# Moving the backward direction's 32x32 substitutions from VectorE to GpSimd, and sharing the output buffers of keys and values

## The chip, the cores and the metric

The kernel runs on one core of a Trainium2 chip. The metric is the time of one execution on the device in microseconds (us); a measurement is the median of several runs. Engines are named as in the profile: PE is TensorE (with PEld, its weight loads), DVE is VectorE, ACT is ScalarE, POOL is GpSimd, and SP is SyncE, whose queue issues nearly all the DMAs. Instructions of one engine run in the order of its program. That order is fixed when the kernel is built: a scheduler lays the instructions out by its own timeline, and in the attention phase the order on PE is the order of the code.

## The reference

One encoder block over 2048 tokens of width 1024. After a norm and one input projection (`z = h @ w_in`), two mixers work side by side, latent attention and a gated linear recurrence that runs once forward and once backward over the tokens. Then come a merge, routing, and 32 experts.

```python
def rwkv_branch(...):
    ...
    y_f = wkv7_scan(r_h, decay_h[:, :, 0], k_dir[:, :, 0], v_h, -kk, kk * a_h[:, :, 0])
    y_b = fl(wkv7_scan(fl(r_h), fl(decay_h[:, :, 1]), ..., fl(-kk), fl(kk * a_h[:, :, 1])))
    ...
def step(state, inp):
    sa = jnp.einsum('bhvk,bhk->bhv', state, a_t)
    state = state * w_t + sa[..., None] * b_t + v_t[..., None] * k_t
    return state, jnp.einsum('bhvk,bhk->bhv', state, r_t)
```

The kernel does the recurrence in chunks of 64 tokens. Each chunk needs the inverse of a unit triangular 64x64 matrix, for 8 heads, 32 chunks and 2 directions.

## The kernel before

**Phase 1** (`phase1`) computes z in column chunks. For each chunk of 128 columns `load_w` (lines 130 to 137) loads the weights, ACT rounds them to `whi`, POOL subtracts to get `wlo` (L136), and PE runs 24 matmuls per 512 tokens (`z_mm`, L143 to L145). The last eight chunks (the gates) run for one block of 512 tokens after the other, and three other pieces of work are threaded between their matmuls:

- `up_kv` and `up_q` project queries, keys and values (matmuls into `u`, copies by DVE and ACT, then a DMA to DRAM). Keys are copied by DVE into `kt` (L586, L587), values by ACT into `vm` (L597, L598), two buffers each.
- `Rwkv.inverses` inverts the triangular matrices in eight **units**, one for each pair (g, d) of a head group g = 0..3 and a direction d (0 forward, 1 backward), in the order (0,0), (0,1), (1,0), ... At most two are live.

One unit (`Rwkv.inverse`) loads the 32x32 diagonal blocks `a` by a DMA on SP's queue (L883), transposes them on DVE (L890), masks them on POOL (L891) and sets the diagonal. Then come **30 substitution steps**: step s multiplies a column by a row into `it` (L898, n*s elements with n = 31 - s) and adds that into `x` (L900), each instruction waiting for the one before. Two DVE transposes follow (L904 into `a`, L905 into `tb`). Then the **tail**: two halves of 16 blocks, each with copies by ACT (L913), 64 small matmuls (L919), a copy (L922), 64 small matmuls (L928), a copy (L931) and a DMA that stores `tt`. The tiles `a`, `of` and `x` exist once for each direction; `it`, `tb`, `tt`, `pe` and the PSUM bank `sa` exist once for both. Because `it` is one buffer, the two live units take turns in their substitutions. Because `a` is used again by the tail, the next unit of a direction loads its `a` only when the tail of the unit before has ended.

**Phase 2** starts with attention's operands for the first head (keys `kh`, `kl`, queries `qhi`, `qlo`, split by ACT and POOL), 16 matmuls for row maxima (L664), and the first scores (L684 to L686, exponentials by ACT at L689, sums on POOL and DVE at L692 and L694). Then the recurrence `rwkv` runs in between the blocks of attention. Its tiles (pool "rw") take the memory of the units' pool, which is closed when the last unit is done; so its loads (L830, L946 to L951, L854) are issued after the last store of `tt`.

```python
        live, todo = [], iter(divmod(u, 2) for u in range(8))
            if len(live) < 2 and (age >= 24 or not live):
        tmp = p.tile([128, 256], F32, name="it", bufs=1)
```

Of the kernel before, what the change touches and what calls it, by code (L numbers as in the profile page):

```python
# [9 lines left out]
F32 = mybir.dt.float32  # L10
# [4 lines left out]
OP = mybir.AluOpType  # L15
# [97 lines left out]
def phase1(k):  # L113

    nc, tc, I, S = k.nc, k.tc, k.I, k.scratch
    with ExitStack() as ctx:
# [142 lines left out]
        with k.psu as k.psu:  # L259
            for b in range(NB):  # L260
                if b == 1:
                    side, more = ExitStack(), 5
                    ups = up_kv(k, side)
                elif b == 2:
                    on(ups, 1000)
                    side.close()
                    side, more = ExitStack(), 2
                    ups = up_q(k, side)
                for j in range(LAST, len(CHUNKS)):
                    load_w(j)  # L270
                    z_out(j, b)
                    on(aside, INV)
                    if b:
                        on(ups, more)
                hx[b].close()
            on(ups, 1000)
            side.close()
            on(aside, 1000)
# [217 lines left out]
def split(k, hi, lo, src, eng=None):  # L496

    k.nc.scalar.copy(hi, src)  # L498
    (eng or k.nc.vector).tensor_tensor(lo, src, hi.bitcast(F32), op=OP.subtract)  # L499


def up_bank(k):
    return k.psu.tile([128, 512], F32, name="u", bufs=3)


def up_w(k, ctx, n, c):

    nc, tc, I = k.nc, k.tc, k.I
    wp = ctx.enter_context(tc.tile_pool(name=n + "w", bufs=1, side="right"))
    whi = wp.tile([128, c, 1024], F32R, name=n + "hi")  # L510
    wlo = wp.tile([128, c, 1024], F32R, name=n + "lo")
    for j in range(c):
        for u in range(2):
            raw = wp.tile([128, 512], F32, name="raw", bufs=RAW)
            sl = slice(u * 512, u * 512 + 512)
            nc.sync.dma_start(raw, I[n][j, :, sl])
            split(k, whi[:, j, sl], wlo[:, j, sl], raw)
    return wp, whi, wlo
# [47 lines left out]
def up_kv(k, ctx):  # L566

    nc, tc, I, S = k.nc, k.tc, k.I, k.scratch
    p, whi, wlo = up_w(k, ctx, "w_ukv", 2)
    for b in range(NB):  # L570
        s = slice(b * 512, b * 512 + 512)
        chi, clo = [], []
        for j in range(2):
            raw = p.tile([128, 512], F32, name="raw", bufs=RAW)
            nc.sync.dma_start(raw, S["ckv"][j, :, s])
            chi.append(p.tile([128, 512], F32R, name="chi", bufs=3))
            clo.append(p.tile([128, 512], F32R, name="clo", bufs=3))
            split(k, chi[j], clo[j], raw)
        for h in range(4):
            t = up_bank(k)  # L580
            c = slice(h * 128, h * 128 + 128)
            for j in range(2):
                nc.tensor.matmul(t, whi[:, j, c], chi[j], start=(j == 0), stop=False)
                nc.tensor.matmul(t, whi[:, j, c], clo[j], start=False, stop=False)
                nc.tensor.matmul(t, wlo[:, j, c], chi[j], start=False, stop=(j == 1))
            kt = p.tile([128, 512], F32, name="kt", bufs=2)  # L586
            nc.vector.tensor_copy(kt, t)  # L587
            nc.sync.dma_start(S["kt"][2 * h:2 * h + 2, :, s], kt)
            yield
        for i in range(4):  # L590
            t = up_bank(k)
            c = slice(i * 128, i * 128 + 128)
            for j in range(2):
                nc.tensor.matmul(t, chi[j][:, c], whi[:, j, 512:], start=(j == 0), stop=False)
                nc.tensor.matmul(t, chi[j][:, c], wlo[:, j, 512:], start=False, stop=False)
                nc.tensor.matmul(t, clo[j][:, c], whi[:, j, 512:], start=False, stop=(j == 1))
            v = p.tile([128, 512], F32, name="vm", bufs=2)  # L597
            nc.scalar.copy(v, t)  # L598
            nc.sync.dma_start(S["vm"][b * 4 + i], v)
            yield  # L600
# [198 lines left out]
class Rwkv:  # L799
# [63 lines left out]
    @staticmethod  # L863
    def row(e, blk):
        return slice(e * 64 + blk * 32, e * 64 + blk * 32 + 32)

    @staticmethod
    def col(blk):
        return slice(blk * 32, blk * 32 + 32)

    def inverse(self, g, d):

        k, p = self.k, self.pi
        nc, S = k.nc, k.scratch
        row, col = self.row, self.col
        q = d
        near, far = (0, 1) if d == 0 else (1, 0)
        turn = lambda t: t.rearrange("p a b -> p b a")  # L880
        a = p.tile([128, 32, 32], F32, name=f"a{q}", bufs=1)
        of = p.tile([128, 32, 32], F32, name=f"of{q}", bufs=1)
        nc.sync.dma_start(a, S["dg"][g, d])  # L883
        for e in range(2):
            nc.sync.dma_start(of[row(e, near)], S["of"][g, row(e, near)])
        yield
        x = p.tile([128, 32, 32], F32, name=f"x{q}", bufs=1)
        tmp = p.tile([128, 256], F32, name="it", bufs=1)

        nc.vector.transpose(turn(x) if d else x, turn(a))  # L890
        nc.gpsimd.affine_select(out=x, in_=x, pattern=[[1, 32], [-1, 32]], base=0, channel_multiplier=0,  # L891
                                compare_op=OP.is_gt, fill=0.0)
        nc.vector.memset(x.rearrange("p a b -> p (a b)")[:, 0:1024:33], 1.0)
        yield
        for s in range(1, 31):
            n = 31 - s
            tv = tmp[:, :n * s].rearrange("p (a b) -> p a b", b=s)
            nc.vector.tensor_tensor(tv, x[:, s + 1:, s:s + 1].to_broadcast([128, n, s]),  # L898
                                    x[:, s:s + 1, 0:s].to_broadcast([128, n, s]), op=OP.mult)
            nc.vector.tensor_tensor(x[:, s + 1:, 0:s], x[:, s + 1:, 0:s], tv, op=OP.add)  # L900
            yield
        ta = p.tile([128, 32, 32], F32, name=f"a{q}", bufs=1)
        tb = p.tile([128, 32, 32], F32, name="tb", bufs=1)
        nc.vector.transpose(turn(ta), turn(x) if d else x)  # L904
        nc.vector.transpose(turn(tb), x if d else turn(x))  # L905
        yield
        for u in range(2):
            js = slice(u * 16, u * 16 + 16)
            tt = p.tile([128, 16, 64], F32, name="tt", bufs=1)
            for e in range(2):  # L910
                nc.gpsimd.memset(tt[row(e, far), :, col(near)], 0.0)
                for blk in range(2):
                    nc.scalar.copy(tt[row(e, blk), :, col(blk)], ta[row(e, blk), js])  # L913
            tv = self.bank("sa").rearrange("p (c t) -> p c t", t=32)
            pe = p.tile([128, 16, 32], F32, name="pe", bufs=1)
            for j in range(16):
                for e in range(2):
                    r, rf = row(e, near), row(e, far)
                    nc.tensor.matmul(tv[rf, j], of[r, u * 16 + j], tb[r, u * 16 + j], start=True, stop=True,  # L919
                                     tile_position=(r.start, rf.start))  # L920
            for e in range(2):
                nc.scalar.copy(pe[row(e, far)], tv[row(e, far)])  # L922
            yield
            tv = self.bank("sa").rearrange("p (c t) -> p c t", t=32)
            for j in range(16):
                for e in range(2):
                    r, rf = row(e, near), row(e, far)
                    nc.tensor.matmul(tv[r, j], pe[rf, j], ta[rf, u * 16 + j], start=True, stop=True,  # L928
                                     tile_position=(rf.start, r.start))
            for e in range(2):  # L930
                nc.scalar.copy(tt[row(e, near), :, col(far)], tv[row(e, near)])  # L931
            nc.sync.dma_start(S["tt"][g, d, :, js], tt)
            yield
# [1004 lines left out]
```

## Time and profile before

| what | value |
|---|---|
| median of 3 runs | 3561.13 us (3556.34 to 3566.02) |
| the profiled execution | 3567.97 us, its span 3566.2 us |
| PE busy | 3245.5 us (91%) |
| DVE busy | 2593.4 us (73%) |
| ACT busy | 1505.7 us (42%) |
| POOL busy | 1400.6 us (39%) |
| granted TensorE clock, mean | 0.956 |

The span runs from the first to the last instruction; the execution's own time lies 1.8 us above it. In the page's 40 slices of some 89 us PE is 90% busy or more nearly everywhere; one exception is the three slices from about 1070 to 1337 us, with 7, 8 and 7 tenths, where phase 1 ends and phase 2 begins. The substitution steps of the eight units run from 932 to 1274 us.

### The profile page before, as it was taken

To read this page: it belongs to the slowest core of one execution; us is meant where nothing else is said; L and a number is where in the kernel's file an instruction comes from. 1 tells how busy PE (TensorE), PEld (TensorE's weight loads), DVE (VectorE), ACT (ScalarE), POOL (GpSimd) and SP (SyncE) were. 2 spreads that over 40 slices of the span, in tenths; PEclk is the share of its full clock that TensorE was granted. 3 is DMA by queue.
4 is the path that set the end of the run, shared out by engine and by line. 5 is a ranking of instruction groups with operands and counts; after the bars stand their busy time and mean duration, and the time that the engine had idled before them with its cause. 6 is when DMAs were issued, how large, how long until landed. Compare 5 with 4: busy or idle time off the path is not lost. (4 is left out here: it accounts for less than half of the span.)

```text
span 3566.2 us, 66955 instructions
## 1 busy us (share of the span) xinstructions
PE 3245.5 (91%) x25104; PEld 2414.4 (68%) x25104; DVE 2593.4 (73%) x4767; ACT 1505.7 (42%) x2866; POOL 1400.6 (39%) x1301
## 2 busy tenths in 40 slices
PE   8999999999997879999999999998789996999990
PEld 6777777777776656666666666664678885666660
DVE  6845677777887767777777777776766765778767
ACT  5322444445443334434434433443322222777762
POOL 1022322333322244545545444544333223665544
PEclk9999999999998879999999999999799997999995
DMA  5544767767554452333333332211544434888887
GB/s 171 177 149 149 233 197 204 205 198 209 188 195 148 132 163 56 94 97 103 103 111 104 105 101 60 54 42 46 189 146 127 150 109 170 329 320 325 332 328 295
DMA packets 392837, 589.71 MB, mean 165 GB/s; under 512 B 66880, under 2 KB 245184, under 8 KB 392512
## 3 DMA queue, kind: packets, MB, share of 16 engines
q1 hardware_dynamic: 380016, 546.36, 48.3%
q0 software_dynamic: 11920, 38.30, 2.9%
q8 instruction: 198, 3.24, 0.4%
q14 instruction: 127, 1.04, 0.1%
q10 hardware_dynamic: 576, 0.76, 0.1%
HBM read 380.78 MB, written 204.51 MB: 164 GB/s over the span
## 5 line engine op out<-in xcount | busy, mean ns | idle before, releaser
L145 PE MATMUL z<-hhi,wlo 128*128 128x512 f32 (+1 forms) x1184 | 469.3, 397 | 3.9 <-POOL wlo L136 3.9
L144 PE MATMUL z<-hlo,whi 128*128 128x512 f32 (+1 forms) x1184 | 470.9, 398 | 0.2 <-DVE hlo L188 0.2
L143 PE MATMUL z<-hhi,whi 128*128 128x512 f32 (+1 forms) x1184 | 468.5, 396 | 1.9 <-ACT hhi L187 1.8
L689 ACT ACTIVATE e<-s 128x512 f32<-128x512 f32 x512 | 304.6, 598 | 375.8 <-PE s L686 352.7
L694 POOL TENSOR_TENSOR acc<-acc,e 128x512 f32<-128x512 f32 x224 | 295.0, 1317 | 338.6 <-ACT e L689 330.2
L665 DVE TENSOR_REDUCE mx<-s 128x1 f32<-128x512 f32 x512 | 337.4, 682 | 46.6 <-PE s L664 44.4
L694 DVE TENSOR_TENSOR accv<-accv,e 128x512 f32<-128x512 f32 x224 | 247.7, 1106 | 53.3 <-ACT e L689 51.1
L136 POOL TENSOR_TENSOR wlo<-wraw,whi 128x1024 fp32r<-128x1024 f32 x61 | 151.0, 2475 | 303.5 <-ACT whi L135 276.0
L145 PEld LDWEIGHTS z<-hhi,wlo 128*128 128x128 f32 (+1 forms) x1184 | 222.4, 188 | 63.6 <-issue 9.0
L144 PEld LDWEIGHTS z<-hlo,whi 128*128 128x128 f32 (+1 forms) x1184 | 222.3, 188 | 56.3 <-issue 3.9
L143 PEld LDWEIGHTS z<-hhi,whi 128*128 128x128 f32 (+1 forms) x1184 | 222.1, 188 | 56.1 <-issue 3.0
L701 PE MATMUL o<-e,v 128*64 128x512 f32 x1024 | 249.6, 609 | 0.0
L498 ACT CAST wh<-wr 128x1024 fp32r<-128x1024 f32 x198 | 204.3, 1047 | 104.9 <-PE y L1639 54.0
L684 PE MATMUL s<-qhi,kh 128*128 128x512 f32 x512 | 210.6, 411 | 38.7 <-ACT e L689 21.7
L499 POOL TENSOR_TENSOR wl<-wr,wh 128x1024 fp32r<-128x1024 f32 x70 | 186.9, 2691 | 124.7 <-ACT wh L498 124.7
L499 DVE TENSOR_TENSOR wl<-wr,wh 128x1024 fp32r<-128x1024 f32 x128 | 185.6, 1456 | 60.8 <-ACT wh L498 55.2
L664 PE MATMUL s<-kh,qhi 128*128 128x512 f32 x512 | 219.6, 435 | 5.6 <-DVE mx L665 4.7
L685 PE MATMUL s<-qlo,kh 128*128 128x512 f32 x512 | 202.8, 396 | 0.0
L686 PE MATMUL s<-qhi,kl 128*128 128x512 f32 x512 | 201.9, 394 | 0.0
L684 PEld LDWEIGHTS s<-qhi,kh 128*128 128x128 f32 x512 | 96.5, 188 | 82.5 <-ACT e L689 38.4
L664 PEld LDWEIGHTS s<-kh,qhi 128*128 128x128 f32 x512 | 97.8, 192 | 55.8 <-DVE mx L665 14.4
L970 DVE TENSOR_TENSOR stk<-sa,mask 64x512 f32<-64x512 f32 x128 | 88.2, 689 | 61.4 <-PE sa L968 59.4
(484 smaller groups left out, 7831.9 us busy)
## 6 DMA issues: line engine op xcount, KB each, us to landing
wr<-w_exp SPq DMA_DIRECT2D x198, 512.0 KB
wraw<-w_in SPq DMA_DIRECT2D x61, 512.0 KB
s_ye<-ye SPq DMA_DIRECT2D x33, 512.0 KB
s_ar<-ar SPq DMA_DIRECT2D x64, 256.0 KB
s_bk<-bk SPq DMA_DIRECT2D x64, 256.0 KB
s_zg<-zo SPq DMA_DIRECT2D x64, 256.0 KB
bk<-s_bk SPq DMA_DIRECT2D x32, 512.0 KB
stk<-s_ar SPq DMA_DIRECT2D x64, 256.0 KB
```

Source lines behind the costliest of these rows:

```text
L143: nc.tensor.matmul(t[:rows], hi[:, c, :rows], hhi[b][:, c], start=(c == 0), stop=False)
L144: nc.tensor.matmul(t[:rows], hi[:, c, :rows], hlo[b][:, c], start=False, stop=False)
L145: nc.tensor.matmul(t[:rows], lo[:, c, :rows], hhi[b][:, c], start=False, stop=(c == 7))
L498: k.nc.scalar.copy(hi, src)
L499: (eng or k.nc.vector).tensor_tensor(lo, src, hi.bitcast(F32), op=OP.subtract)
L664: nc.tensor.matmul(t, B.qhi[:, i * 128:(i + 1) * 128], KT[B.h][0][b], start=True, stop=True)
L665: nc.vector.tensor_reduce(B.mx[:, i, b:b + 1], t, axis=AX.X, op=OP.max)
L684: nc.tensor.matmul(t, khi[b][:, c], B.qhi, start=True, stop=False)
L685: nc.tensor.matmul(t, khi[b][:, c], B.qlo, start=False, stop=False)
L689: nc.scalar.activation(e, t, AF.Exp, scale=scale)
L694: eng.tensor_tensor(a, a, e, op=OP.add)
L701: nc.tensor.matmul(B.o[r], VT[B.h][:, 2 * u + i], B.e[u][i], start=(u == 0), stop=(u == NT // 2 - 1))
```

## The change

Three edits. The temporary of the substitution becomes two tiles, one for each direction. In a unit of the backward direction all 60 instructions of the substitution go to GpSimd; those of the forward direction stay on VectorE. Keys and values share one ring of three output buffers in place of two rings of two. The lines behind the first edits move down by two (L898 becomes L900, L919 becomes L921, and so on).

```diff
@@ up_kv
-            kt = p.tile([128, 512], F32, name="kt", bufs=2)
+            kt = p.tile([128, 512], F32, name="kv", bufs=3)
             nc.vector.tensor_copy(kt, t)
...
-            v = p.tile([128, 512], F32, name="vm", bufs=2)
+            v = p.tile([128, 512], F32, name="kv", bufs=3)
             nc.scalar.copy(v, t)
@@ Rwkv.inverse
-        tmp = p.tile([128, 256], F32, name="it", bufs=1)
+        tmp = p.tile([128, 256], F32, name=f"it{q}", bufs=1)
+
+        eng = nc.gpsimd if d else nc.vector
...
         for s in range(1, 31):
             n = 31 - s
             tv = tmp[:, :n * s].rearrange("p (a b) -> p a b", b=s)
-            nc.vector.tensor_tensor(tv, x[:, s + 1:, s:s + 1].to_broadcast([128, n, s]),
-                                    x[:, s:s + 1, 0:s].to_broadcast([128, n, s]), op=OP.mult)
-            nc.vector.tensor_tensor(x[:, s + 1:, 0:s], x[:, s + 1:, 0:s], tv, op=OP.add)
+            eng.tensor_tensor(tv, x[:, s + 1:, s:s + 1].to_broadcast([128, n, s]),
+                              x[:, s:s + 1, 0:s].to_broadcast([128, n, s]), op=OP.mult)
+            eng.tensor_tensor(x[:, s + 1:, 0:s], x[:, s + 1:, 0:s], tv, op=OP.add)
             yield
```

The scheduler lays the program out anew, and the end of the eight units falls at another place. The names below carry tile numbers; `a_12116`, `x_12123`, `it_12124`, `a_12466` and `of_12117` belong to the last unit, (3,1), and `zo` is the output of a z block.

SP's queue at the end of phase 1, before: the load of the last unit's `a`, then the stores of z, then the first keys of attention.

```order
L562 DMA s_qt<-qf 2x64x512
L883 DMA a_12116<-s_dg 128x1024
L932 DMA s_tt<-tt 128x1024
L164 DMA s_zg<-zo 128x512
L132 DMA wraw<-w_in 128x1024
L562 DMA s_qt<-qf 4x32x512 x2
L164 DMA s_zg<-zo 128x512 x4
L932 DMA s_tt<-tt 128x1024
L635 DMA e<-s_kt 64x512
```

The same place now:

```order
L164 DMA s_zg<-zo 128x512 x2
L934 DMA s_tt<-tt 128x1024
L164 DMA s_zg<-zo 128x512
L885 DMA of_12117<-s_of 32x1024 x2
L164 DMA s_zg<-zo 128x512
L883 DMA a_12116<-s_dg 128x1024
L934 DMA s_tt<-tt 128x1024
L635 DMA e<-s_kt 64x512
```

Before, five stores of z and the last load of weights came behind that load; now it comes behind the last store of z.

POOL's program, now, where the first exponentials of attention are summed (L692, L694). Before, the mask of the last unit (L891) stood ahead of the last two `wlo` (L136), and no substitution was on POOL.

```order
L913 MEMSET tt 32x16x32 x2
L902 TENSOR_TENSOR x_12123<-x_12123,it_12124 128x28x3
L900 TENSOR_TENSOR it_12124<-x_12123 128x108
L692 COPY acc<-e 128x512
L902 TENSOR_TENSOR x_12123<-x_12123,it_12124 128x27x4
L694 TENSOR_TENSOR acc<-acc,e 128x512
L900 TENSOR_TENSOR it_12124<-x_12123 128x130
L902 TENSOR_TENSOR x_12123<-x_12123,it_12124 128x26x5
L900 TENSOR_TENSOR it_12124<-x_12123 128x150
L902 TENSOR_TENSOR x_12123<-x_12123,it_12124 128x25x6
```

The first eight of the last unit's 60 substitution instructions lie between attention's splits and sums; from `L900 ... 128x130` on, 52 of them follow one another with nothing between, and behind them come a memset of `tt` and the recurrence's first memset.

PE's program from the last scores ahead of the recurrence, before and now:

```order
L686 MATMUL s<-qhi_12679,kl_12645 128x512
L968 MATMUL sa<-stk,bk 64x128 x16
L990 MATMUL sa<-cst,bks 128x64 x16
L1003 MATMUL sa<-stk,bk 64x64 x16
L968 MATMUL sa<-stk,bk 64x128 x8
```

```order
L686 MATMUL s<-qhi_12679,kl_12645 128x512
L921 MATMUL sa<-tb,of_12117 32x32 x32
L930 MATMUL sa<-a_12466,pe 32x32 x32
L921 MATMUL sa<-tb,of_12117 32x32 x32
L930 MATMUL sa<-a_12466,pe 32x32 x32
L970 MATMUL sa<-stk,bk 64x128 x16
L992 MATMUL sa<-cst,bks 128x64 x16
```

The last unit's four groups of small matmuls were spread over the 16 matmuls for row maxima; now they stand together behind the first four scores, directly ahead of the recurrence.

## Rows read from the trace of the kernel before

**Rows 1.** Busy time by stretch: length, then each engine's busy time (instructions), clock, DMA.

```profile
932.00:1272.00 340.00, 291.96 (x2669) 230.04 (x2670) 276.51 (x570) 127.94 (x200) 83.72 (x61) 0.91 0.46 154
1272.00:1336.00 64.00, 42.06 (x598) 31.43 (x594) 31.23 (x54) 25.63 (x44) 34.67 (x50) 0.63 0.74 199
1336.00:1400.00 64.00, 63.60 (x680) 44.09 (x675) 49.14 (x81) 26.11 (x50) 31.46 (x28) 1.00 0.27 73
```

**Rows 2.** Timeline of PE: start, duration, operation; the hand-over between the phases.

```profile
1270.70 0.39 PE L145 MATMUL z<-hhi,wlo 128*128 128x512 f32 x1
...
1336.18 0.50 PE L664 MATMUL s<-kh,qhi 128*128 128x512 f32 x1
```

**Rows 3.** Source line of the multiply: count, shortest, median and longest in ns.

```profile
L898 DVE TENSOR_TENSOR it<-x x240: 158/360/2607, 932.4 to 1274.1; 128x30 f32<-128x30 f32 x8, 128x84 f32<-128x84 f32 x8, 128x130 f32<-128x130 f32 x8, 128x168 f32<-128x168 f32 x8
```

**Rows 4.** Timelines of POOL and DVE where a POOL operation meets substitution steps.

```profile
935.45 2.51 POOL L136 TENSOR_TENSOR wlo<-wraw,whi 128x1024 fp32r<-128x1024 f32 x1 [1.47 <-ACT whi L135]
935.62 2.47 DVE L898 TENSOR_TENSOR it<-x 128x108 f32<-128x108 f32 x1
...
938.90 0.30 DVE L898 TENSOR_TENSOR it<-x 128x130 f32<-128x130 f32 x1
939.24 0.30 DVE L900 TENSOR_TENSOR x<-x,it 128x130 f32<-128x130 f32 x1
```

**Rows 5.** The same timelines where a DVE operation came first.

```profile
1104.98 1.30 POOL L560 TENSOR_TENSOR qf<-qf,qr 128x512 f32<-128x512 f32 x1 [10.21 <-DVE qr L559]
1111.23 0.68 DVE L499 TENSOR_TENSOR clo<-raw,chi 128x512 fp32r<-128x512 f32 x1
1111.40 1.65 POOL L560 TENSOR_TENSOR qf<-qf,qr 128x512 f32<-128x512 f32 x1 [5.12 <-DVE qr L559]
1111.83 1.47 DVE L900 TENSOR_TENSOR x<-x,it 128x228 f32<-128x228 f32 x1
```

**Rows 6.** Timeline of POOL: operations nearest in kind to the moved ones.

```profile
712.91 0.65 POOL L436 TENSOR_TENSOR q<-cs 128x260 f32<-128x260 f32 x1 [6.11 <-DVE cs L434]
713.52 0.92 POOL L469 TENSOR_TENSOR ks<-ks,kd 128x256 f32<-128x256 f32 x1
...
714.54 0.73 POOL L482 TENSOR_TENSOR ks<-ks,zr 128x256 f32<-128x256 f32 x1
...
1318.46 1.05 POOL L980 TENSOR_TENSOR bks<-bk,wc 128x512 f32<-128x512 f32 x1 [4.00 <-DMA bk<-s_bk]
```

**Rows 7.** Timelines of DVE and POOL: unit (0,0)'s tail begins; unit (1,0) starts.

```profile
971.19 2.08 DVE L904 STREAM_TRANSPOSE a<-x 128x1024 f32<-128x1024 f32 x1
...
1008.61 1.27 POOL L891 TENSOR_SCALAR_AFFINE_SELECT x<-x 128x1024 f32<-128x1024 f32 x1 [6.36 <-DVE x L890]
```

**Rows 8.** Timelines of SP and DVE: the last unit's load and start.

```profile
1241.60 2.02 DVE L890 STREAM_TRANSPOSE x<-a 128x1024 f32<-128x1024 f32 x1 [14.86 <-DMA a<-s_dg]
1254.59 17.61 SPq L164 DMA_DIRECT2D s_zg<-zo  x4
1274.30 0.19 DVE L900 TENSOR_TENSOR x<-x,it 128x30 f32<-128x30 f32 x1
```

**Rows 9.** Timeline of POOL: the second sum of the first scores.

```profile
1311.86 1.59 POOL L694 TENSOR_TENSOR acc<-acc,e 128x512 f32<-128x512 f32 x1
```

**Rows 10.** Timelines of DVE, PE, ACT and SP: the last unit's end, then the recurrence's loads.

```profile
1276.41 2.07 DVE L905 STREAM_TRANSPOSE tb<-x 128x1024 f32<-128x1024 f32 x1
1299.47 1.92 PE L928 MATMUL sa<-a,pe 32*32 32x32 f32 x64 [1.19 <-ACT pe L922]
1301.87 2.50 ACT L913 COPY tt<-a 32x512 f32<-32x512 f32 x4 [0.71 <-DMA s_tt<-tt]
1304.38 1.17 ACT L931 COPY tt<-sa 32x512 f32<-32x512 f32 x2
1305.61 0.34 SPq L932 DMA_DIRECT2D s_tt<-tt  x1
1308.30 0.35 SPq L830 DMA_DIRECT2D mask<-mask  x1
```

## The prediction, made before the changed kernel had run

> **What bounds the kernel now.** I read the stretches first, then PE's timeline at the hand-over from phase 1 to phase 2, then the substitution steps on DVE and what they meet on POOL, and last the chain that starts the recurrence. In phase 1's last 340 us, from 932 to 1272, PE is busy 291.96 us at a granted clock of 0.91 [rows 1]. At the full clock that work is some 266 us, so about 74 us of the stretch is PE waiting or slowed. In the next 64 us, PE has 42 us of work at 0.63; from 1336 on it is full at 1.00 [rows 1]. The last z matmul ends at 1271.1, and 65.1 us later, at 1336.2, PE is back at full rate [rows 2]. From there on PE's program is the same in both kernels and PE bound it, so I price two things: when z ends (call it Z), and how long the hand-over lasts.
>
> The 480 substitution instructions run from 932 to 1274 us on DVE [rows 3]. A middling one takes 0.30 us and the next starts 0.04 us after it; one that meets `wlo` on POOL takes 2.47 us, nearly all of POOL's 2.51 [rows 4]. The reverse happens too: with a DVE subtraction under way, a POOL addition took 1.65 instead of 1.30, and the DVE step issued next to it took 1.47 [rows 5]. Two such operations do not run together; whichever is second waits.
>
> The hand-over hangs on the last unit. Its `a` arrived at 1241.6, its substitution ran under the last four z blocks and ended at 1274.5, 3 us after z [rows 8]. Its tail gave the last store at 1305.6, and only then, at 1308.3, could the recurrence's loads be issued [rows 10]; 28 us later PE is full.
>
> **What the change does, part by part.**
>
> *The price of a step on POOL.* No row has this operation there. An addition of two plain operands took 0.73 us at 256 elements and 1.30 at 512 [rows 5, 6], so 0.15 us and 2.23 ns an element. With one operand broadcast it took 0.65 at 260 and 1.05 at 512 [rows 6], so 0.24 us and 1.59 ns. A unit has 30 of each, and n*s summed over its steps is 4960: 30 x 0.24 + 4960 x 1.59 ns = 15.1 us for the multiplies, 30 x 0.15 + 4960 x 2.23 ns = 15.6 us for the additions. Between two steps I take 0.07 us, between DVE's 0.04 [rows 4] and the 0.10 from L469's end to the start of L482, which needs its result [rows 6]. That is 31 + 4 = **35 us for a unit on POOL**. Ends: 32 us without gaps; 51 us if short rows cost half as much again as the long ones I have rows for.
>
> *Holding.* Where a forward unit runs on DVE at the same time, each step can wait for the other engine's. On POOL that is from 0 to one DVE step of some 0.40 us; I take 0.20, 12 us a unit, with 0 and 24 as the ends. On DVE a step waits for the rest of a POOL step, much as before it waited for `wlo`.
>
> *The backward chain up to the end of z.* It starts at about 934. Unit (0,1): 35 + 12 + five `wlo` that the new order puts between its steps, 5 x 2.5 = 60 us, to 994. From a unit's last step to the next unit's mask it took 39 us, 971.2 to 1009.9 [rows 7], which I keep; because the forward unit ends at nearly the same time and `tb`, `tt` and `sa` exist once, I add half a tail, 15: 1048. Unit (1,1): POOL's order puts the mask of the third forward unit behind 36 of its steps. The forward chain reaches that at 990 + 39 + 30 (60 steps at about 0.40 and some copies) + 39 = 1098; the 24 steps behind take 19 us, and one `wlo` and one addition 4: 1121. Then 39: 1160. Unit (2,1): 47 + four `wlo` (10) + three additions of queries (4) = 61: 1221. PE's order threads the last 57 z matmuls through this unit's tail, some 30 us: **Z at 1251 instead of 1271, 20 us earlier.** Ends: PE's own floor, 932 + 266 = 1198; and with full holding, 24 us more over units (0,1) and (2,1), 1275.
>
> *The last unit.* Its load now stands behind the last store of z, so none of its substitution lies under z any more. POOL's order lets eight steps trickle in between attention's splits and the first sums, and puts 52 behind the second L694. That sum ended 42.4 us after z before [rows 2, 9], held there by attention's loads, row maxima and scores, which wait for z's end in both programs; I keep 42.4. The 52 steps: 26 x 0.24 + 4680 x 1.59 ns + 26 x 0.15 + 4680 x 2.23 ns + 52 x 0.07 = 32 us, with nothing else on DVE or PE. Then two transposes, 4.0 us [rows 8, 10], and the tail alone: four groups of matmuls at 1.92 and four copies at 1.17, 12.4 us; the second half's copies into `tt` (2.5 us) wait for the first half's store and mostly fit beside; the last store takes 2.7 us and 0.1 to issue, so 20 us in all [rows 10]. Then the loads, 27.9 us from 1308.3 to full rate [rows 2, 10]. Sum: 42.4 + 32 + 20 + 28 = **122 us against 65.1, 57 us more.** The work that hid this substitution was z; its cover is gone, and PE, whose order has these four groups ahead of everything else, waits.
>
> *Output buffers.* Three for keys and values in place of four cost nothing while a store lands before the third next copy. At worst I put 15 us, on a PE with 74 us to spare; zero in the sum, 15 in the range. The DVE time freed shows nowhere by itself: it only lets z come earlier.
>
> **Sum.** 57 - 20 = +37 us. The profiled execution took 3567.97, so 3605; the shown median is 6.8 us below that, so **3598 us**, 1.0% slower. Differences under 0.3% (11 us) I call no change.
>
> **The rivals.**
>
> *The two engines serialise (slower still).* If every step of one engine waits for a whole one of the other, POOL's 12 us of holding become 24 in two units, Z falls back to 1275 and the change is +61: 3622 us. For it: the 2.47 against 0.30, and 1.47 and 1.65 in a row [rows 4, 5]. Against: the forward and backward units overlap for only part of their time in the new order. The Trainium skill (Perfetto Trace Analysis, Optimizing Scalar/DVE Operations) speaks against the change in this very sense: since the two share an SBUF port, "offloading operations between those two might not help"; by that rule z would end no earlier, as in this rival, and the rows on holding agree with it.
>
> *POOL's short rows are dearer.* At half as much again, a unit costs 16 us more, in the last one fully exposed: 3598 + 16 = 3614 with z's cover for the rest, up to 3640 where (2,1) pushes z as well. The nearest rows have long rows; the moved operations have rows of 1 to 30 elements.
>
> *The parallel chains win (faster).* PE waited or ran slow for 74 us. The one `it` buffer made eight substitutions take turns; now two chains run. If holding is slight and a tail with its load takes 25 us, not 39, then unit (2,1) ends by about 1168, z meets PE's floor at 1198, and 57 - 73 = -16: 3545 us. It decides at a gain in z of 57 us: Z before 1214. Against it: tails depend on SP's and PE's order and on one `tt`, none of which the change widens; and the backward chain must run four substitutions, now on the slower engine.
>
> *No change.* Z between 1203 and 1225 pays for the hand-over: 3561.
>
> That the change does not do what it says is ruled out only in part: the order shows units (0,0) and (0,1) side by side, but (1,1) mostly beside a forward tail and (3,1) beside nothing.
>
> **How the numbers follow.** My case, Z from 1240 to 1262 (3587 to 3609 and the neighbours of that): 0.47. Serialised: 0.18; dear rows: 0.12; faster: 0.11; no change: 0.12. So slower 0.77, same 0.12, faster 0.11. The range 3550 to 3640 leaves out most of the faster case and some 0.08 beyond dear rows and late buffers together. With Z at its floor and at 1275 plus 16 us of dear steps the sum gives 3545 and 3638, which is what the range rests on.
>
> **What would show it.** Right: an L902 row on POOL ending some 75 us after the last z, about 52 of them back to back at 0.5 to 0.7 us; PE idle from the first scores until L921; z ending at 1240 to 1262; substitution rows on DVE well above 0.30 while POOL's run. Wrong: z before 1214; POOL's steps much shorter than 0.55 us on average; or the recurrence's loads issued before the last unit's store. The forecast fails as a whole if PE reaches full rate before about 1350 us.

## The result and the profile after

The changed kernel took 3621.56 us (median of 4 runs, 3617.80 to 3626.45) against 3561.54 us for the kernel before (4 runs); the ratio is 1.0175 [1.0161, 1.0190]. It is slower, by 60 us where 37 were forecast; 3621.6 lies in the range.

The profiled execution has a span of 3616.1 us, 49.9 above that of before, while the medians differ by 60.0. The difference of 10 us lies behind the hand-over: from the 33rd matmul of row maxima (L664), which I use as a marker below, to the end took 2210 us in this execution and 2217 to 2227 us in all thirteen others shown here. At the marker itself the two traces are 61 us apart (1345.0 and 1406.1).

Busy time by stretch, with the columns of [rows 1]:

```profile
932.00:1272.00 340.00, 289.43 (x2414) 228.91 (x2415) 208.76 (x336) 120.52 (x188) 178.62 (x238) 0.89 0.45 150
1272.00:1336.00 64.00, 28.56 (x435) 19.65 (x431) 23.43 (x35) 21.44 (x37) 52.66 (x85) 0.65 0.32 95
1336.00:1400.00 64.00, 25.30 (x428) 21.79 (x429) 11.12 (x15) 12.52 (x22) 14.96 (x30) 0.52 0.54 136
1400.00:1464.00 64.00, 63.60 (x680) 43.95 (x680) 49.69 (x82) 26.86 (x52) 31.98 (x30) 1.00 0.23 62
```

Up to 1272, VectorE gave up 68 us and GpSimd took on 95, and PE did no more than before: 289.43 us against 291.96 [rows 1]. PE reaches full work at clock 1.00 one whole stretch of 64 us later; in between it is busy 25.30 us, at 0.52, close to the lower of its two levels.

Timeline of PE at the hand-over (start, duration, operation, idle time before it and what ended that), to compare with [rows 2, 10]:

```profile
1274.93 0.39 PE L145 MATMUL z<-hhi,wlo 128*128 128x512 f32 x1
...
1347.76 1.92 PE L921 MATMUL sa<-tb,of 32*32 32x32 f32 x64 [38.10 <-DVE tb L907]
1350.94 1.92 PE L930 MATMUL sa<-a,pe 32*32 32x32 f32 x64 [1.26 <-ACT pe L924]
1354.12 1.91 PE L921 MATMUL sa<-tb,of 32*32 32x32 f32 x64 [1.27 <-ACT tt L933]
1362.44 1.92 PE L930 MATMUL sa<-a,pe 32*32 32x32 f32 x64 [6.40 <-ACT pe L924]
...
1397.28 0.50 PE L664 MATMUL s<-kh,qhi 128*128 128x512 f32 x1
```

z ends at 1275.3, 4 us later than before, not 20 earlier. Then PE stands for 38.10 us at the last unit's L921, and is at full rate 122.0 us after z, where before it took 65.1.

What it stood for, on GpSimd and SP, against [rows 8, 9, 10]:

```profile
1276.52 0.37 SPq L883 DMA_DIRECT2D a<-s_dg  x1
...
1311.30 1.26 POOL L694 TENSOR_TENSOR acc<-acc,e 128x512 f32<-128x512 f32 x1
1312.52 0.44 POOL L900 TENSOR_TENSOR it<-x 128x130 f32<-128x130 f32 x1
...
1343.65 0.25 POOL L902 TENSOR_TENSOR x<-x,it 128x30 f32<-128x30 f32 x1
...
1358.72 1.09 POOL L913 MEMSET tt<- 32x512 f32 x2 [14.82 <-DMA s_tt<-tt]
...
1368.35 0.33 SPq L830 DMA_DIRECT2D mask<-mask  x1
```

The last unit's load goes out at 1276.52, after z. Behind the second sum 52 steps run back to back, for 31.4 us in which neither PE nor VectorE nor ACT nor a DMA is at work. The recurrence's loads start 24.5 us after the last step.

The eight units, from the first to the last row of their 60 steps (us; busy time of the steps in brackets):

| unit | VectorE, forward | unit | GpSimd, backward |
|---|---|---|---|
| (0,0) | 932.6 to 981.7 (38.0) | (0,1) | 934.2 to 1002.8 (33.0) |
| (1,0) | 1018.6 to 1051.1 (25.2) | (1,1) | 1047.6 to 1120.9 (33.4) |
| (2,0) | 1097.5 to 1146.5 (28.5) | (2,1) | 1178.8 to 1251.2 (31.6) |
| (3,0) | 1216.0 to 1257.4 (33.2) | (3,1) | 1297.9 to 1343.9 (30.6) |

A unit on GpSimd is busy 31 to 33 us, but the first three stretch over 69 to 73. What GpSimd waited for between the steps of unit (2,1), 1178 to 1252 us (us in total, times, longest):

```profile
POOL qf L560 <- DVE qr L559: 8.3, 1, 8.3
POOL x L893 <- DVE x L892: 6.1, 1, 6.1
POOL tt L913 <- DMA s_tt<-tt: 5.9, 1, 5.9
```

None of these waits belongs to the unit. They are those of instructions that stand in GpSimd's program between its steps: an addition of queries, the mask of the *forward* unit, a memset of `tt`. In unit (0,1) it is `wlo` that waits, until ACT has rounded the weights; ACT's rounding (L135) in turn waited most for PE's z matmuls, 20.4 us in 8 waits between 920 and 1280 us. GpSimd's wait from 930 to 1005 us:

```profile
POOL wlo L136 <- ACT whi L135: 17.3, 3, 9.4
```

How the two engines met, on DVE and POOL, in unit (2,1) beside unit (3,0); the first line is VectorE's form with no step on GpSimd, the last GpSimd's with no step on VectorE:

```profile
1023.73 0.35 DVE L902 TENSOR_TENSOR x<-x,it 128x184 f32<-128x184 f32 x1
...
1228.08 0.66 POOL L902 TENSOR_TENSOR x<-x,it 128x220 f32<-128x220 f32 x1
1228.24 0.70 DVE L902 TENSOR_TENSOR x<-x,it 128x184 f32<-128x184 f32 x1
1228.81 0.55 POOL L900 TENSOR_TENSOR it<-x 128x210 f32<-128x210 f32 x1
1228.98 0.61 DVE L900 TENSOR_TENSOR it<-x 128x198 f32<-128x198 f32 x1
...
1333.08 0.65 POOL L902 TENSOR_TENSOR x<-x,it 128x220 f32<-128x220 f32 x1
```

VectorE's step takes 0.70 instead of 0.35 and falls into GpSimd's rhythm; GpSimd's takes 0.66 beside VectorE and 0.65 alone. Between these two streams the holding is all on one side.

### The profile page after: what moved, and what is told of

It reads as the page before. It is cut to its first block, busy times and chain, and to the rows that moved or that the text cites. A ratio compares the mean times of both kernels' runs of the same rounds, so it can differ in the third digit from the quotient of the medians.

```text
span 3616.1 us, 66951 instructions
## 1 busy us (share of the span) xinstructions
PE 3251.1 (90%) x25104; PEld 2422.1 (67%) x25104; DVE 2523.4 (70%) x4527; ACT 1506.0 (42%) x2866; POOL 1526.3 (42%) x1541
## 5 line engine op out<-in xcount | busy, mean ns | idle before, releaser
L694 POOL TENSOR_TENSOR acc<-acc,e 128x512 f32<-128x512 f32 x224 | 294.6, 1315 | 340.7 <-ACT e L689 332.5
L694 DVE TENSOR_TENSOR accv<-accv,e 128x512 f32<-128x512 f32 x224 | 247.8, 1106 | 50.7 <-ACT e L689 48.6
L136 POOL TENSOR_TENSOR wlo<-wraw,whi 128x1024 fp32r<-128x1024 f32 x61 | 152.3, 2498 | 234.0 <-ACT whi L135 197.0
L499 POOL TENSOR_TENSOR wl<-wr,wh 128x1024 fp32r<-128x1024 f32 x70 | 186.8, 2689 | 124.9 <-ACT wh L498 124.8
L499 DVE TENSOR_TENSOR wl<-wr,wh 128x1024 fp32r<-128x1024 f32 x128 | 185.5, 1455 | 60.8 <-ACT wh L498 56.3
L664 PE MATMUL s<-kh,qhi 128*128 128x512 f32 x512 | 219.3, 434 | 5.0 <-DVE mx L665 4.4
L664 PEld LDWEIGHTS s<-kh,qhi 128*128 128x128 f32 x512 | 97.4, 191 | 55.3 <-DVE mx L665 14.6
```

Source lines behind the costliest of these rows:

```text
L664: nc.tensor.matmul(t, B.qhi[:, i * 128:(i + 1) * 128], KT[B.h][0][b], start=True, stop=True)
L694: eng.tensor_tensor(a, a, e, op=OP.add)
```

## The experiments

**Theory A**, that of the prediction: time is lost because the last backward unit falls behind z, where its steps and tail are bare; it falls there because the chain of backward units is slow on GpSimd, whose program puts other, waiting instructions between the steps. **Theory B**: the two engines hold each other's steps, so nothing is won by running them side by side. **Theory C**: the buffers (the ring of three, the two temporaries) cost something by themselves. Each version has runs of the kernel before taken beside it, and its ratio is to those.

**The engine alone undone.**

```diff
-        eng = nc.gpsimd if d else nc.vector
+        eng = nc.vector
```

> All eight units' substitutions on VectorE again, but with one temporary per direction and the shared ring of three kept; so the one edit undone is the engine. Theory A (the last backward unit lost z's cover because the chain of backward units became slow on GpSimd): the last unit's load is issued ahead of the last z stores again, z ends near 1271, the hand-over is near 65 us, and the time is that of before, 3555 to 3570. Theory B (the two engines hold each other up): the same time, since GpSimd has no steps; B and A are not told apart here. Theory C (the ring of three buffers, or two temporaries, cost something by themselves): a good part of the 60 us stays, over 3580.

Measured 3567.42 us, ratio 1.0010 [1.0001, 1.0020]; z ends at 1272.0, full rate 65.8 us later. C falls: ring and temporaries together cost at most 7 us. The whole loss comes with the engine.

**The forward substitution left out.**

```diff
-        for s in range(1, 31):
+        for s in range(1, 31 if d else 1):
```

> The forward direction's 240 substitution instructions are left out (its masked blocks go on as they are), the backward ones stay on GpSimd; VectorE no longer runs beside them. Theory A: a backward unit's 60 steps are as busy as before, 30 to 33 us, the last unit still has 52 steps behind the second sum of attention, the hand-over stays at 115 to 125 us, and the time is 3600 to 3625, what is gained being waits on forward units only. Theory B: the steps on GpSimd get shorter, by 10 us or more in units (0,1) and (2,1), z ends 20 to 24 us earlier, and the time is at or under 3598.

One run, 3595.9 us. The four backward units were busy 32.1, 33.5, 30.7 and 30.3 us, against 33.0, 33.4, 31.6 and 30.6 with VectorE running beside them: B's shorter steps did not appear, and the hand-over stayed at 120.3 us, as A has it. But z ended at 1244.7, 30.6 us earlier, and the time is B's. The gain came through waits. Over unit (2,1), now 55.4 us long (1165.2 to 1220.7), GpSimd waited for

```profile
POOL tt L913 <- DMA s_tt<-tt: 4.8, 2, 2.5
POOL qf L560 <- DVE qr L559: 0.2, 1, 0.2
```

5.0 us where it had been 20.3: with VectorE free, `qr` was there at once, and the forward mask no longer stood among the steps. So VectorE does matter, in a way that neither theory had. A reading that fits is a loop: GpSimd's steps hold VectorE's, VectorE is late with `qr` and the forward transposes, and GpSimd's own program waits for those. How much of the 30 us is this loop and how much the mere absence of the forward steps this run can't divide.

**The last unit alone back on VectorE.**

```diff
-        eng = nc.gpsimd if d else nc.vector
+        eng = nc.gpsimd if d and g < 3 else nc.vector
```

> Only the last backward unit (3,1) goes back to VectorE; the first three stay on GpSimd. Theory A: the chain up to the last unit's load is as in the changed kernel (load behind the last store of z, z ends at about 1275); its 60 steps then take about 25 us on a free VectorE from about 1298, not 46 with the wait behind attention's sums, so the last step ends near 1323 instead of 1344 and the time is 3595 to 3605. Theory B: what costs is the holding in the first three units, which stays; the last unit ran beside nothing, and would only gain its 6 us of price: 3612 to 3618.

Measured 3618.68 us (3602.72 to 3624.04 in 4 runs), ratio 1.0142 [1.0113, 1.0170]. A's number missed, and B's 3612 to 3618 is the nearer one. The steps were busy 26.8 us but took from 1294.0 to 1339.4 and ended only 4.5 us sooner than on GpSimd, because VectorE isn't free there. Its timeline:

```profile
1300.66 1.22 DVE L900 TENSOR_TENSOR it<-x 128x108 f32<-128x108 f32 x1
...
1305.72 1.87 DVE L665 TENSOR_REDUCE mx<-s 128x1 f32<-128x512 f32 x3
1307.52 0.86 DVE L900 TENSOR_TENSOR it<-x 128x150 f32<-128x150 f32 x1
1308.30 1.87 DVE L665 TENSOR_REDUCE mx<-s 128x1 f32<-128x512 f32 x3
```

Attention's row maxima stand between the steps, the step of 1.22 us runs beside GpSimd's splits of attention's operands (L499), and the second sum itself slipped to 1325.1. Once the unit is behind z, either engine has attention's work in its program there.

**The last two backward units back on VectorE** (`g < 2` in the same line).

> Backward units (0,1) and (1,1) stay on GpSimd, (2,1) and (3,1) go back to VectorE. Theory A: unit (2,1) no longer waits in GpSimd's queue and takes 35 to 50 us, the last load is out before the last stores of z again, the hand-over falls to 65 to 85 us, and the time is 3555 to 3585. Theory B: two of the three units that ran beside forward units still hold VectorE, so at least half of z's delay stays and VectorE has four more units of its own: 3585 to 3610.

Measured 3576.55 us, ratio 1.0031 [1.0017, 1.0046]. Unit (2,1) took 46.5 us, the last load went out at 1255.15, ahead of the last z stores, and the hand-over was 67.4 us. Two units still ran on GpSimd, 69.6 and 73.9 us long, and that cost 12 us, where B expects over 20: A's reading. With the last unit back under z, four fifths of the loss are gone.

**A load that doesn't wait for the tail.** The next unit's `a` goes into the tile that `x` leaves.

```diff
-        a = p.tile([128, 32, 32], F32, name=f"a{q}", bufs=1)
+        a = p.tile([128, 32, 32], F32, name=f"a{q}", bufs=2)
...
-        x = p.tile([128, 32, 32], F32, name=f"x{q}", bufs=1)
+        x = p.tile([128, 32, 32], F32, name=f"a{q}", bufs=2)
...
-        ta = p.tile([128, 32, 32], F32, name=f"a{q}", bufs=1)
+        ta = p.tile([128, 32, 32], F32, name=f"a{q}", bufs=2)
```

> The changed kernel, but a and x of one direction share a ring of two tiles: the next unit's a is loaded into the tile that x leaves after the transposes, and no longer waits for the tail (whose copy of x is in the other tile). In the order, 37 instead of 52 steps of the last unit stand behind the second sum of attention. Theory A (chain of backward units: tail and load between units, then waits in GpSimd's queue): the steps of one unit start 15 to 30 us sooner after the last step of the one before, z ends between 1235 and 1265, 37 steps cost about 22 us after the sum, the hand-over is about 113 us, and the time 3580 to 3605. Theory B (the two engines hold each other, the order is not what matters): units overlap more, are held more, z stays near 1275; only the 15 steps are saved: 3608 to 3615.

Measured 3610.98 us, ratio 1.0137 [1.0118, 1.0155]. From the last step of one backward unit to the first of the next it took 39.3, 51.1 and 37.4 us in place of 44.8, 57.9 and 46.6: 5 to 9 us sooner, not 15 to 30. z ended at 1266.4, the hand-over was 110.7 us, and the time is B's. What A has acts at a third of the size that I gave it: the load is a small part of what lies between two units, and the masks and memsets that wait in GpSimd's program stay.

**`wlo` off GpSimd.**

```diff
-            nc.gpsimd.tensor_tensor(lo, raw, hi.bitcast(F32), op=OP.subtract)
+            (nc.vector if j >= 27 else nc.gpsimd).tensor_tensor(lo, raw, hi.bitcast(F32), op=OP.subtract)
```

> The changed kernel, but from weight chunk 27 on wlo is subtracted on VectorE, so that no step on GpSimd queues behind a wlo and the wait for its weights; 28 instead of 52 steps stand behind the second sum. Theory A (in-order waits on GpSimd lengthen the units): unit (0,1) loses its 17 us of waits for whi and the subtractions, 55 us or less instead of 69, z ends 5 to 25 us earlier, the hand-over is about 108 us, and the time 3580 to 3602. Theory B: VectorE is what is short, held by GpSimd's steps: with 33 subtractions more it falls behind, z ends no earlier and the time is at or over 3608.

Measured 3592.35 us, ratio 1.0074 [1.0058, 1.0089]: z at 1254.6, the hand-over 107.8 us, unit (0,1) 43.8 us, (1,1) 45.6, (2,1) 49.6 instead of 68.6, 73.3 and 72.5. In unit (0,1) nothing is waited for any more between the steps. All of A's numbers held; B's did not, though VectorE carries the subtractions. They are not dear there:

```profile
L136 DVE TENSOR_TENSOR wlo<-wraw,whi x21: 1173/1225/1715, 934.3 to 1243.8; 128x1024 fp32r<-128x1024 f32 x21
```

1.23 us (the median) against 2.41 on GpSimd, where one had held a VectorE step for as long [rows 4]. The first three units gained 23 to 28 us each; the first two gaps between them grew (to 68 and 65 us; in the first, memsets of `tt` wait 36.2 us for stores), so z gained 21.

**Both edits together.**

> Both edits (wlo on VectorE from chunk 27 on, and the ring of two for a and x) in the changed kernel; 20 steps behind the second sum. Theory A: the gains add in part, z ends at 1225 to 1260, the 20 steps cost 12 us, the hand-over is about 103 us, and the time 3560 to 3590. Theory B: no better than the ring alone, 3600 or more.

Measured 3583.12 us, ratio 1.0046 [1.0030, 1.0062]; z at 1254.3, the hand-over 100.6 us. As A has it, and still slower than before: 20 steps are bare.

**All on VectorE, with the ring of two, laid out earlier.** The engine line as in the first experiment, the three lines of the ring, and `INV`, the number of pieces of the units' code that are laid out for each z block:

```diff
-INV = 7
+INV = 9
```

> All substitutions on VectorE, one temporary for each direction, the ring of two for a and x, and the units' code laid out at 9 pieces per z block instead of 7, which puts the last tail's stores earlier between the stores of z. Theory A (what counts is how long after z the last tail ends): the last unit's steps end 10 to 25 us before z's end instead of 3 to 10 after it, the hand-over falls from 65 to 40 to 55 us, and the time is 3535 to 3555, better than both kernels. Against it: if z's own end is bound by VectorE, z ends later by as much, and the time stays at 3560 to 3568.

Measured 3552.69 us, ratio 0.9964 [0.9952, 0.9977]: better than both kernels. The last step ends at 1259.8, 11 us before z's end at 1270.9, and the recurrence's loads start at 1291.3 instead of 1308.3. Of these 17 us the marker keeps 8. The three edits were not tried one by one in this version.

**Only unit (0,1) on GpSimd**, with the ring of two and `INV = 9` (`g < 1` in the engine's line).

> Only unit (0,1) on GpSimd, the ring of two for a and x, 9 pieces per z block; VectorE has one unit less to do than in the version with all on VectorE. Theory A: what a unit on GpSimd costs is paid only where it comes late; (0,1) has z ahead of it for 270 us, so the chain gains VectorE time, the last unit's steps end near 1245 instead of 1260, z ends at 1262 to 1271, the hand-over is 50 to 57 us, and the time is 3538 to 3553. Theory B: the steps of (0,1) hold VectorE for as long as they save it, and the time is 3550 to 3562.

Measured 3557.98 us, ratio 0.9986 [0.9974, 0.9997]: B's number. Unit (0,0) beside it was busy 38.0 us on VectorE, 24.2 when both were on VectorE; of the 23.7 us that (0,1) took there, VectorE got back 10. The last step ended at 1251.3, 22 us before z, and nothing came of it. z ended at 1273.6, and the hand-over has another end by then, on SP and PE:

```profile
1282.52 2.66 SPq L830 DMA_DIRECT2D mask<-mask  x1
...
1306.58 0.59 SPq L655 DMA_DIRECT2D e<-s_qt  x1
...
1315.53 4.47 PE L664 MATMUL s<-kh,qhi 128*128 128x512 f32 x9 [8.20 <-ACT qhi L498]
```

The recurrence's loads now stand ahead of attention's second load of queries (L655), which was issued at 1280.59 before, and PE waits for it. From z to the marker it took 65.8 us with the last step 11 us ahead of z's end, and 64.4 with 22 (the kernel before: 73.9).

**Two units on GpSimd, without `wlo`**: `g < 2`, `wlo` on VectorE, the ring of two, `INV = 9`.

> Units (0,1) and (1,1) on GpSimd, the other six on VectorE, wlo on VectorE from chunk 27 on, the ring of two for a and x, 9 pieces per z block. Theory A: GpSimd's two units run without wlo between their steps, z ends at 1250 to 1262, the last unit's steps end before that or at most 15 us after, the hand-over is 57 to 75 us, and the time is 3540 to 3562. Against it: VectorE now has six units and 33 wlo, its forward chain is late, and z ends at 1270 or later: 3560 to 3575.

Measured 3550.79 us, ratio 0.9950 [0.9937, 0.9963], the lowest ratio of all; its interval overlaps that of all on VectorE, so that the two units on GpSimd gain anything over that version is not shown. All on VectorE with `wlo` there too was not tried. z ends at 1261.7, 9.4 us earlier than before, and PE is at full rate 54.9 us later, a little under what A gave. Its busy times in the stretch from 1272 to 1336:

```profile
1272.00:1336.00 64.00, 54.29 (x581) 39.00 (x581) 40.02 (x67) 23.16 (x42) 34.70 (x40) 0.79 0.69 175
```

**The kernel before with `INV = 9` alone.**

> The kernel before with one number changed: 9 pieces of the units per z block instead of 7. In the order the last four stores of tt come after 60, 62, 64 and 64 of the 64 gate blocks, not all after the last. Theory A (what counts is how long after z the last tail ends): the last store of tt moves some 10 to 15 us forward, the hand-over falls to 50 to 60 us, and the time is 3548 to 3558. If it is the units' chain itself that is late, the new order makes PE wait for the tail ahead of z, z ends later by as much, and the time stays at 3560 to 3566.

Measured 3562.76 us, ratio 0.9984 [0.9974, 0.9994]. The last store of `tt` came 11 us sooner (1294.5) and the hand-over fell to 54.2 us, as A has it, but the marker came only 2 us sooner and A's time missed. So the order of the tails by itself is worth little. The trace says where the rest went, on SP, ACT and PE:

```profile
1322.69 0.47 SPq L635 DMA_DIRECT2D raw<-s_kt  x1
...
1332.43 1.14 ACT L498 CAST kh<-raw 96x512 fp32r<-96x512 f32 x2 [11.87 <-DMA raw<-s_krr]
...
1334.65 0.80 PE L684 MATMUL s<-qhi,kh 128*128 128x512 f32 x1 [6.68 <-ACT e L689]
```

The recurrence's loads now stand ahead of attention's next keys (L635 and L636, issued from 1294.52 on before). ACT waits for those keys, the exponentials behind that in its program are late, and PE, already at full rate, waits 6.68 us for them. The same wait of PE is 5.73 us with all on VectorE, the ring and `INV = 9`.

**Two units on GpSimd, with `wlo` back on GpSimd** (the version of ratio 0.9950 with this one edit undone).

> The fastest version so far (two backward units on GpSimd, the ring of two for a and x, 9 pieces per z block) with one edit undone: wlo stays on GpSimd. Theory A (steps on GpSimd that queue behind a wlo pay for its weights' wait, and that is what makes z late): units (0,1) and (1,1) take 60 to 75 us again instead of some 45, z ends at 1268 to 1278 instead of 1262, and the time is 3558 to 3570. Against it: if the order of the last units alone made the gain, the time is 3548 to 3555.

Measured 3562.44 us, ratio 0.9998 [0.9988, 1.0007]: the gain is gone. Units (0,1) and (1,1) took 69.2 and 67.6 us again, against 43.7 and 46.3; z ended at 1270.6, which is 9 of the 13 us that the marker lost. GpSimd's waits from 930 to 1115 us have as the largest

```profile
POOL wlo L136 <- ACT whi L135: 31.6, 5, 9.8
```

A's numbers held. What of the gain is the wait and what the shorter subtraction, which no longer holds VectorE's steps from GpSimd, this pair doesn't divide.

All that compute the same, in one table (z's end and the last substitution step in us; then from z's end to the marker):

| version | ratio to before | z ends | last step | z to marker |
|---|---|---|---|---|
| before | 1 | 1271.1 | 1274.5 | 73.9 |
| before, INV 9 | 0.9984 | 1271.4 | 1270.6 | 71.3 |
| changed | 1.0175 | 1275.3 | 1343.9 | 130.8 |
| all on VectorE | 1.0010 | 1272.0 | 1281.5 | 74.9 |
| last unit on VectorE | 1.0142 | 1277.9 | 1339.4 | 122.3 |
| last two on VectorE | 1.0031 | 1279.8 | 1290.4 | 76.3 |
| changed, ring of two | 1.0137 | 1266.4 | 1324.5 | 119.5 |
| changed, `wlo` on VectorE | 1.0074 | 1254.6 | 1307.1 | 116.7 |
| changed, both | 1.0046 | 1254.3 | 1302.3 | 109.5 |
| all on VectorE, ring, INV 9 | 0.9964 | 1270.9 | 1259.8 | 65.8 |
| (0,1) on GpSimd, ring, INV 9 | 0.9986 | 1273.6 | 1251.3 | 64.4 |
| (0,1), (1,1) on GpSimd, `wlo` on VectorE, ring, INV 9 | 0.9950 | 1261.7 | 1264.6 | 63.7 |
| the same, `wlo` on GpSimd | 0.9998 | 1270.6 | 1269.4 | 67.8 |

## Why the prediction was right in sign and 24 us short

- **Where the time lies.** 3621.6 is outside the 3587 to 3609 of my own case; the range holds it through the room that it left for the rivals.
- **What bounds it.** Right: z's end and the hand-over moved the marker by 61 us; behind it the traces agree within the 17 us told above, and what makes these is not shown.
- **The price on GpSimd.** Right: 31 us of steps were forecast, 30.6 to 33.4 measured; 32 us for the 52 bare steps, 31.4 measured. The rival of dearer short rows is out: a step of 30 elements takes 0.24 us. Two slips carried nothing: without gaps the forecast's terms give 31 us, not 32, and VectorE's middling step is 0.36 us by [rows 3], not 0.30.
- **The last unit.** Right term by term within 5 us, and to the microsecond in the sum only by luck: 42.4 + 32 + 20 + 28 = 122 forecast, 37.2 + 31.4 + 24.5 + 28.9 = 122.0 measured. The sum on GpSimd ended 5 us sooner than I kept it, and the tail took 4.5 longer: I had ACT's copies of the second half mostly fit beside the first half's store, as before [rows 10], where they waited 0.71 us for it, and here they waited 4.65:

```profile
1358.71 2.50 ACT L915 COPY tt<-a 32x512 f32<-32x512 f32 x4 [4.65 <-DMA s_tt<-tt]
```

- **Holding.** Wrong in place. I put 12 us on GpSimd in two units; the run without forward steps puts it at 0 to 1 us. It fell on VectorE: unit (0,0) was busy 38.0 us, 24.4 with both directions on VectorE. The Trainium skill (SBUF — State Buffer, SBUF: two separate sides) says that of a VectorE operation with two inputs in SBUF and a GpSimd operation that reads SBUF, the one that starts first keeps the shared port pair for the whole instruction and the other blocks. The trace agrees in both orders (2.47 us on VectorE beside GpSimd's 2.51 [rows 4]; 1.65 on GpSimd in place of 1.30, behind VectorE's operation [rows 5]). It also shows what the rule leaves to the reader: of these two chains of like steps it was the one with the shorter step that waited.
- **The step that failed: the backward chain up to the end of z.** Until 1121 it came out to the microsecond, in part by luck: unit (1,1) was to start at 1048 and end at 1121, and did at 1047.6 and 1120.9, but unit (0,1) had ended at 1002.8, not 994, and the gap behind it was 44.8 us, not 54. Then came "Then 39: 1160", and "47 + four `wlo` (10) + three additions of queries (4) = 61: 1221". Measured were 58 to the next unit's first step and 72.5 for the unit, so it ended at 1251.2 instead of 1221. z ended 24 us behind that, where I had 30: 1275.3 instead of 1251, 24 us, the whole miss, and outside the 1240 to 1262 that I had named as the sign of being right. The 39 us were those of a tail on its own [rows 7]. Here the tail's second half waited for a store of `tt`, the load of the next `a` went out only when the tail's last matmuls had ended, and a `wlo` and a memset stand ahead of the unit's first step:

```profile
1155.91 2.50 ACT L915 COPY tt<-a 32x512 f32<-32x512 f32 x4 [8.41 <-DMA s_tt<-tt]
...
1164.35 0.32 SPq L883 DMA_DIRECT2D a<-s_dg  x1
...
1171.75 2.10 DVE L892 STREAM_TRANSPOSE x<-a 128x1024 f32<-128x1024 f32 x1 [5.56 <-DMA a<-s_dg]
...
1175.16 2.40 POOL L136 TENSOR_TENSOR wlo<-wraw,whi 128x1024 fp32r<-128x1024 f32 x1
1177.62 1.08 POOL L913 MEMSET tt<- 32x512 f32 x2
1178.78 0.25 POOL L900 TENSOR_TENSOR it<-x 128x30 f32<-128x30 f32 x1
```

  And in the unit I priced the instructions that the order puts between the steps at their durations, and not at what they themselves wait for: 20.3 us here, for an addition of queries, a mask and a memset. The 12 us of holding in the 61, which did not come, hid a part of that. With `wlo` off GpSimd z ended at 1254.6, near the forecast.
- **The rival of two engines that serialise** gave 3622 us and z at 1275, both as measured, and not by its mechanism: it put 24 us of holding on GpSimd, where there is at most one. Part of it may be right in a form that it did not have: holding on VectorE that comes back to GpSimd through `qr` and the forward mask, which no run divides from the rest. By the rule of the Trainium skill named with it (Perfetto Trace Analysis, Optimizing Scalar/DVE Operations), z would end no earlier. It did not, at 1275.3 against 1271.1.
- **Output buffers.** Right at zero within 7 us.

## What to carry to other kernels

A step that is moved to another engine takes its place in that engine's program, and pays not only for the instructions between its steps but for whatever those wait for: look up the idle time in front of each of them in the trace before pricing it. A chain that is off the bound costs little (12 us with the first two units on GpSimd) until its last link drops out from under the work that covers it; then its steps, its tail and the loads behind it are all bare. By the medians, bringing the last two links back gave 48 of the 60 us and taking the waiting work (`wlo`) off the engine 32, while cheaper steps for the last unit alone, where it stands, gave 6. Once another chain ends last, finishing still earlier is worth little: no version came under 63.7 us from z to the marker, and in all four whose last step ended before z, loads of attention had fallen behind the recurrence's on SP's queue. No version moved substitutions to GpSimd and was shown to be faster than the best with all of them on VectorE.

## What was not expected of the hardware

These two streams of dependent steps on VectorE and GpSimd do not share the loss: VectorE's took 0.61 to 0.70 us instead of 0.35 to 0.37, GpSimd's took 0.66 us against 0.65 alone for the same form. GpSimd is held too where VectorE's operation is the long one: with `wlo` on VectorE, in the version of ratio 0.9950,

```profile
941.48 1.58 DVE L136 TENSOR_TENSOR wlo<-wraw,whi 128x1024 fp32r<-128x1024 f32 x1
...
942.05 1.45 POOL L902 TENSOR_TENSOR a<-a,it 128x198 f32<-128x198 f32 x1
```

a step that takes 0.58 us alone (1335.71 in the changed kernel) took 1.45, and unit (0,1) was busy 39.0 us instead of 33.0. It ended 28 us sooner than in the changed kernel all the same.
